# Sample attention of a hybrid decoder step: small matmuls moved into separate row and column tiles of the TensorE array

## The chip, the cores and the metric

The kernel is one program on one core of a Trainium2 chip. The metric is the device time in microseconds (us) of one execution; three runs of the kernel before gave 2195.8, 2200.24 and 2203.21, median 2200.24. Everything is computed in float32, in one launch.

## The reference, cut to what matters

The model is one inference step of a two-layer trunk: layer 0 with gated linear attention (GLA, four heads), layer 1 with sliding-window attention; in both a memory cross attention (four heads of 64) stands beside it, and SwiGLU feed-forward networks before and after. It runs on 512 prompt tokens and on 32 sample tokens (8 sequences of 4 new tokens, each sequence with its own past state or cache). The change is about three pieces of the work on the sample tokens:

```
# GLA, sample: per sequence b and head h, states S (96 x 192)
S = exp(g_t)[..., None] * S + k_t[..., :, None] * v_t[..., None, :]
o_t = einsum('bhk,bhkv->bhv', q_t, S)
# memory attention: keys and values of 256 memory tokens per sequence
s = einsum('blhd,bmhd->bhlm', q, mk) * 64 ** -0.5
o = einsum('bhlm,bmhd->blhd', softmax(s), mv)
```

The kernel computes the GLA recurrence of the four new tokens in closed form: output = (score matrix of the new tokens) times v, plus (decayed q) times the old state; new state = decay times old state plus (decayed k) transposed times v.

## The kernel before, in words

Activations stand transposed: features on the 128 partitions, tokens in the columns. Half 0 holds 256 prompt tokens and the 32 sample tokens (288 columns), half 1 the other 256. Dense products run on TensorE (PE) as three fp32r matmuls per block (`dense`, L356, and `product`, L342). The matmuls of the attention are float32 and each is two instructions on PE, so "x16" of such a line in the trace is eight matmuls.

Around the change the work of layer 0 is as follows. `in_a` projects half 0 to q, k, v and r; the v blocks are turned from features to tokens by transposes on PE (L805, 128 columns each; the sample block has 32 tokens). Then `weave` runs `attend_a` of half 0 (`attn_a` for GLA with `mem_prompt` and `mem_sample` for the memory heads) against a filler of dense work of half 1: the end of its first feed-forward, then its RMSNorm (`enter`: sums on PE at L400, `rstd`, a broadcast on PE at L412, the scaled and split inputs at L434, L298 and L299), then its own `in_a`. The filler's dense matmuls are what PE does while the attention waits, except between the last feed-forward product and the first projection, where the RMSNorm stands between them.

`attn_a` first makes the scores of the four heads (`gla_scores`; the decayed keys are turned at L929), then calls `gla_out` per head. There the prompt chunks come first (L953 to L966), then, for half 0, the sample part of that head, all of it on the 32 sample tokens:

- L976: eight masked copies of the keys (32 x 96 each, one per sequence), L980: eight masked copies of q (96 x 32).
- L983: one matmul scores x v, L990: eight matmuls masked q x old state, all into rows 0 to 31 of one PSUM bank (the stationary operand is 96 rows by 32 columns, 192 columns are streamed). The states are loaded for a pair of heads at the even head (L987), into eight buffers of the pool `ld`.
- L998: eight matmuls masked keys x v (32 rows by 96 columns, 192 streamed), L999: the new state on VectorE (DVE), and at the odd head its store (L1002).

`mem_sample` runs once per layer (l = 0 and 1). After the softmax, L715 masks the transposed probabilities of all four heads for one sequence, and L718 multiplies them (128 x 128) with the value block of all four heads (256 columns), 16 matmuls in all; of the 128 x 256 result only the four 32 x 64 diagonal blocks are kept (L724).

The order of the instructions on each engine is set when the kernel is built, by a scheduler that simulates the engines' times and takes priorities (`high_priority`); so an edit in one place moves instructions of other lines as well. On the chip each engine goes through its list in order and waits on semaphores.

Of the kernel before, what the change touches and what calls it, by code (L numbers as in the profile page):

```python
# [15 lines left out]
ALU = mybir.AluOpType  # L16
# [3 lines left out]
P = 128  # L20
# [36 lines left out]
def constants():  # L57
# [25 lines left out]
    bmt = (tok[:, None] // LS == np.arange(NB)[None]).astype(np.float32)  # L83
# [149 lines left out]
class Build:  # L233
# [126 lines left out]
    def copy(self, out, ps, scale=1.0):  # L360
        with self.tc.high_priority(offset=self.AHEAD):
            self.nc.scalar.activation(out, ps, AF.Copy, scale=scale)
        return out

# [311 lines left out]
    def mem_sample(self, l, mq, mo):  # L676
# [34 lines left out]
        for b in range(NB):  # L711
# [11 lines left out]
        for h in range(4):  # L723
            nc.scalar.activation(o[NS * h:NS * h + NS], po[NS * h:NS * h + NS, 64 * h:64 * h + 64], AF.Copy)  # L724
# [26 lines left out]
    def blocks(self, h):  # L751
        return ((0, P, 0), (P, P, 1)) + (((2 * P, NS, 2),) if h == 0 else ())

    def in_a(self, h, xs, s):
# [42 lines left out]
        for hp in range(2):  # L797
# [4 lines left out]
            for a, m, c in self.blocks(h):  # L802
                pv = self.bd() if h else self.bt()
                for j in range(3):
                    nc.tensor.transpose(pv[:m, j * P:(j + 1) * P], vf[j][:, a:a + m], self.ident)  # L805
                t = self.v("vtok")
                nc.scalar.activation(t[:m].rearrange("p a b -> p (a b)"), pv[:m, :2 * GV], AF.Copy)
# [13 lines left out]
    def attn_a(self, h, s):  # L821
# [7 lines left out]
        for i in range(GH):  # L829
            yield from self.gla_out(h, i, s, ss)  # L830
        s.tmp.close()
# [20 lines left out]
    def gla_scores(self, h, i, s):  # L852
# [75 lines left out]
        for a, n, c in self.blocks(h):  # L928
            nc.tensor.transpose(pk[:n, c * GK:(c + 1) * GK], kd[:, a:a + n], self.ident[:GK, :GK])  # L929
        nc.scalar.activation(kt[:, :2].rearrange("p a b -> p (a b)"), pk[:, :2 * GK], AF.Copy)  # L930
        if h == 0:
            nc.scalar.activation(kt[:NS, 2], pk[:NS, 2 * GK:3 * GK], AF.Copy)
# [4 lines left out]
    def gla_out(self, h, i, s, ss):  # L937
# [7 lines left out]
        def finish(po, n, c):  # L945
            nc.scalar.activation(o[c][:n], po, AF.Copy)
            junk = s.tmp.u(GV)
            nc.scalar.activation(junk[:n], po, AF.Square, accum_out=ss[:n, 4 * c + i:4 * c + i + 1])

        for c in range(2):  # L950
# [5 lines left out]
            finish(po[:, :GV], P, c)  # L956
# [11 lines left out]
        if h == 1:  # L968
            nc.sync.dma_start(d["o_gp"][i], self.state[i])
            self.drop(self.state[i], at, qe, kt)  # L970
            return

        kb, kbs = [], [self.u(shape=(2, GK), rows=NS) for _ in range(NB // 2)]
        for g in range(0, NB, 2):
            t = kbs[g // 2]
            nc.vector.tensor_tensor(out=t, in0=kt[:NS, 2].unsqueeze(1).to_broadcast([NS, 2, GK]),  # L976
                                    in1=self.bmt[:, g:g + 2].unsqueeze(2).to_broadcast([NS, 2, GK]), op=ALU.mult)
            kb += [t[:, 0], t[:, 1]]
        qb = self.u(shape=(NB, NS), rows=GK)
        nc.vector.tensor_tensor(out=qb, in0=self.bm[:GK], in1=qe[:, SC].unsqueeze(1).to_broadcast([GK, NB, NS]),  # L980
                                op=ALU.mult)
        po = self.bt()
        nc.tensor.matmul(po[:NS, :GV], ats, v[2][:NS], start=True, stop=False)  # L983
        for j in range(NB):
            if i % 2 == 0:
                st = self.ld("st", [P, 2, GV])[:GK]
                nc.sync.dma_start(st, d["state"][j, i // 2].rearrange("p (a v) -> p a v", a=2))  # L987
                self.st[j] = st
            st = self.st[j][:, i % 2, :]
            nc.tensor.matmul(po[:NS, :GV], qb[:, j, :], st, start=False, stop=j == NB - 1)  # L990
        finish(po[:NS, :GV], NS, 2)
        yield
        for j in range(0, NB, 2):
            pn = self.bt()
# [477 lines left out]
```

## Time and profile before

| | us |
|---|---|
| median of the three runs | 2200.24 |
| the profiled execution, its own time | 2195.54 |
| its span, first to last instruction | 2193.8 |
| PE busy in the span (share) | 2127.1 (97%) |
| DVE busy (share) | 1544.0 (70%) |
| ScalarE (ACT) busy (share) | 1067.2 (49%) |
| mean granted clock of TensorE | 0.981 of full speed |

The two sample attentions lie at 416 to 700 us (layer 0, half 0, woven with dense work of half 1) and at 1580 to 1720 us (layer 1). A PE instruction counts as busy from its start to the modelled end of its result, so consecutive ones overlap, and "busy" says that PE had something in flight, not that its array was full.

### The profile page before, as it was taken

Reading aid. Unit: us, or ns where it says so; the run is one execution under the profiler, and the core shown is the slowest. Engines: PE = TensorE matmul, PEld = TensorE weight load, DVE = VectorE, ACT = ScalarE, POOL = GpSimd, SP = SyncE. Lnnn points to the kernel's source line nnn. Section 1 sums busy time; section 2 is a strip of 40 time slices with the busy share of each in tenths; the row PEclk is TensorE's granted clock in tenths of the full one; section 3 lists DMA queues with packets and bytes.
Section 4 is the critical chain, followed back from the end, with each engine's and each line's share of the span. In section 5 each row is a group of like instructions: output and inputs, shape, how many; then the busy total and the mean of one; then the engine's idle time right before and its main releaser. Section 6 shows DMA issues by size and latency. Waiting matters only on the chain.

```text
span 2193.8 us, 40498 instructions
## 1 busy us (share of the span) xinstructions
PE 2127.1 (97%) x16166; PEld 2035.5 (93%) x16166; DVE 1544.0 (70%) x3246; ACT 1067.2 (49%) x2101; POOL 36.3 (2%) x69
## 2 busy tenths in 40 slices
PE   7999999999999998999999999999999999999998
PEld 6999999998789988999999999999987889999998
DVE  7886665587467868858577776665776876966755
ACT  5554444654446555525355554444443445544434
POOL 5000000000000000000000000000000000000000
PEclk9999999999899999999999999999999999999999
DMA  7533253434344432333354533243443333232344
GB/s 231 159 100 116 70 170 116 138 128 140 107 139 155 138 108 95 109 95 95 119 160 151 179 100 107 78 144 121 145 130 113 122 117 116 96 114 80 106 138 135
DMA packets 90398, 273.00 MB, mean 124 GB/s; under 512 B 11312, under 2 KB 25152, under 8 KB 90176
## 3 DMA queue, kind: packets, MB, share of 16 engines
q1 hardware_dynamic: 89632, 269.87, 39.1%
q8 instruction: 127, 2.08, 0.4%
q14 instruction: 63, 0.52, 0.1%
q10 hardware_dynamic: 576, 0.52, 0.1%
HBM read 264.04 MB, written 7.70 MB: 124 GB/s over the span
## 4 chain that ended last, share of the span: by engine, by line
PE 83%; DVE 8%; DMA 4%; issue 2%; ACT 1%; SPq 0%; DVEq 0%; ACTq 0%
PE bank L356 54%; PE bank L342 18%; PE bank L878 1%; PE bank L1103 1%; DMA u19r<-gu_ffn 1%; DMA u20r<-gu_ffn 1%; DMA u21r<-gu_ffn 1%; DMA u18r<-gu_ffn 1%; PE bank L645 1%; PE bank L998 1%; PE bank L990 1%; PE bank L1117 1%; PE bank L1116 1%; DVE u L299 1%; PE bank L666 1%
## 5 line engine op out<-in xcount | busy, mean ns | idle before, releaser
L298 ACT ACTIVATE u<-u 128x272 fp32r<-128x272 f32 (+3 forms) x328 | 133.3, 421 | 121.7 <-DVE u L533 47.6
L299 DVE TENSOR_TENSOR u<-u,u 128x272 fp32r<-128x272 f32 (+3 forms) x328 | 137.3, 429 | 8.2 <-ACT u L298 7.1
L541 DVE SCALAR_TENSOR_TENSOR x<-bank,x 128x16 f32<-128x16 f32 (+2 forms) x192 | 59.6, 342 | 115.4 <-PE bank L356 114.6
L356 PE MATMUL bank<-u,d0h 128*128 128x272 f32 (+2 forms) x352 | 71.6, 290 | 0.0
L356 PE MATMUL bank<-u,d1h 128*128 128x272 f32 (+2 forms) x352 | 70.8, 288 | 0.0
L356 PE MATMUL bank<-u,d2h 128*128 128x272 f32 (+2 forms) x352 | 68.4, 289 | 0.4 <-DVE x L741 0.4
L356 PE MATMUL bank<-u,d3h 128*128 128x272 f32 (+2 forms) x352 | 68.3, 290 | 0.0
L356 PE MATMUL bank<-u,d4h 128*128 128x272 f32 (+2 forms) x352 | 67.3, 288 | 0.0
L356 PE MATMUL bank<-u,d5h 128*128 128x272 f32 (+2 forms) x352 | 67.1, 288 | 0.0
L356 PE MATMUL bank<-u,d7h 128*128 128x272 f32 (+2 forms) x352 | 67.0, 288 | 0.0
L356 PE MATMUL bank<-u,d6h 128*128 128x272 f32 (+2 forms) x352 | 66.8, 288 | 0.0
L530 ACT ACTIVATE u<-u 128x272 f32<-128x272 f32 x56 | 24.1, 430 | 71.4 <-DVE u L529 71.4
L356 PEld LDWEIGHTS bank<-u,d0h 128*128 128x128 f32 x352 | 56.3, 188 | 0.2
L356 PEld LDWEIGHTS bank<-u,d1h 128*128 128x128 f32 x352 | 56.2, 188 | 0.0
L356 PEld LDWEIGHTS bank<-u,d2h 128*128 128x128 f32 x352 | 55.4, 188 | 0.7 <-issue 0.5
L356 PEld LDWEIGHTS bank<-u,d3h 128*128 128x128 f32 x352 | 55.5, 188 | 0.3 <-DVE x L576 0.3
L356 PEld LDWEIGHTS bank<-u,d4h 128*128 128x128 f32 x352 | 55.3, 188 | 0.4 <-issue 0.3
L356 PEld LDWEIGHTS bank<-u,d5h 128*128 128x128 f32 x352 | 55.1, 188 | 0.2
L356 PEld LDWEIGHTS bank<-u,d7h 128*128 128x128 f32 x352 | 55.1, 188 | 0.1
L356 PEld LDWEIGHTS bank<-u,d6h 128*128 128x128 f32 x352 | 55.2, 188 | 0.0
L356 PE MATMUL bank<-u,d1l 128*128 128x272 f32 (+2 forms) x176 | 50.8, 289 | 0.0
L356 PE MATMUL bank<-u,d4l 128*128 128x272 f32 (+2 forms) x176 | 50.7, 288 | 0.0
(1179 smaller groups left out, 7792.1 us busy)
## 6 DMA issues: line engine op xcount, KB each, us to landing
g0r<-gu_ffn SPq DMA_DIRECT2D x8, 512.0 KB, 3.3
u0r<-gu_ffn SPq DMA_DIRECT2D x8, 512.0 KB, 3.4
g1r<-gu_ffn SPq DMA_DIRECT2D x8, 512.0 KB, 3.5
u1r<-gu_ffn SPq DMA_DIRECT2D x8, 512.0 KB, 3.9
g2r<-gu_ffn SPq DMA_DIRECT2D x8, 512.0 KB, 3.4
u2r<-gu_ffn SPq DMA_DIRECT2D x8, 512.0 KB, 3.3
g3r<-gu_ffn SPq DMA_DIRECT2D x8, 512.0 KB, 3.4
u3r<-gu_ffn SPq DMA_DIRECT2D x8, 512.0 KB, 3.4
```

Source lines behind the costliest of these rows:

```text
L298: nc.scalar.activation(h, src, AF.Copy)
L299: nc.vector.tensor_tensor(out=l, in0=src, in1=h.bitcast(F32), op=ALU.subtract)
L342: self.nc.tensor.matmul(ps, a[:, k, :], x, start=start and k == 0 and j == 0, stop=k == len(xs) - 1 and j == 2, skip_group_check=True)
L356: self.nc.tensor.matmul(ps, w[:, k, :], x, start=i == 0 and j == 0, stop=i == kc - 1 and j == 2)
L530: nc.scalar.activation(c2, c2, AF.Silu)
L541: nc.vector.scalar_tensor_tensor(out=x, in0=p, scalar=0.5, in1=x, op0=ALU.mult, op1=ALU.add)
L645: nc.tensor.matmul(ps[:, b, :], mq[b][rows, tok], kt[b][rows], start=True, stop=True)
L666: nc.tensor.matmul(po[rows, (h // 2) * P:][:, :P], v[mt][:, 64 * h:64 * h + 64], pt[h][:, mt, :], start=mt == 0, stop=mt == 1)
L878: nc.tensor.matmul(pv[:, c * half:(c + 1) * half], lhs[:, c * P:(c + 1) * P], second(rhs[:, c * P:(c + 1) * P]), start=True, stop=True)
L990: nc.tensor.matmul(po[:NS, :GV], qb[:, j, :], st, start=False, stop=j == NB - 1)
L998: nc.tensor.matmul(pv[:, e], kb[j + e], v[2][:NS], start=True, stop=True)
L1103: nc.tensor.matmul(dst, self.vt[n - i][:, 64 * kv:64 * kv + 64], t.rearrange("p g t -> p (g t)"), start=i == 0, stop=i == last)
```

## The change

The matmuls of the three pieces are cut or regrouped so that neighbours in the instruction list use different row or column tiles of the array. `side_by_side` keeps the scheduler from reordering the TensorE instructions inside it among themselves.

- Memory heads: the 16 matmuls 128 x 128 by 256 columns per layer become 64 of 128 x 32 by 64 columns; four of them (one per head) write rows 0, 32, 64 and 96 of the same bank. The four copies of L724 become one.
- GLA, sample part: it leaves `gla_out` and becomes `gla_sample`, called once for two heads, after both heads' prompt parts. The q x state matmuls of the two heads alternate between column tiles (output rows 0 to 31 and 32 to 63). The masked keys now stand on all 128 partitions (the 32 tokens repeated four times), one mask per two groups of sequences, and the keys x v matmuls alternate between two row tiles and two PSUM banks. The second moment is taken from the copied output instead of PSUM.
- For this, the 32-token blocks of v and of the keys must stand four times on the partitions: `turn` replaces one transpose of such a block by four matmuls with the identity, into output rows 0, 32, 64 and 96.

```diff
+    def side_by_side(self):
+        return self.tc.manual_schedule(engines={self.nc.tensor.engine})
...
             for mt in range(2):
-                nc.tensor.matmul(po[:, :MT], pt[:, 4 * mt:4 * mt + 4].rearrange("p a t -> p (a t)"), vc[:, mt, :],
-                                 start=b == 0 and mt == 0, stop=b == NB - 1 and mt == 1)
+                with self.side_by_side():
+                    for h in range(4):
+                        nc.tensor.matmul(po[NS * h:NS * h + NS, :64], pt[:, 4 * mt + h, :], vc[:, mt, 64 * h:64 * h + 64],
+                                         start=b == 0 and mt == 0, stop=b == NB - 1 and mt == 1)
...
-        for h in range(4):
-            nc.scalar.activation(o[NS * h:NS * h + NS], po[NS * h:NS * h + NS, 64 * h:64 * h + 64], AF.Copy)
+        nc.scalar.activation(o, po[:, :64], AF.Copy)
...
+    def turn(self, out, t, ident):
+        m = t.shape[1]
+        if m == P:
+            self.nc.tensor.transpose(out, t, ident)
+        else:
+            with self.side_by_side():
+                for a in range(0, P, m):
+                    self.nc.tensor.matmul(out[a:a + m], t, ident, start=True, stop=True)
...
-                    nc.tensor.transpose(pv[:m, j * P:(j + 1) * P], vf[j][:, a:a + m], self.ident)
+                    self.turn(pv[:, j * P:(j + 1) * P], vf[j][:, a:a + m], self.ident)
...
             yield from self.gla_out(h, i, s, ss)
+            if h == 0 and i % 2:
+                yield from self.gla_sample(i // 2, s, ss)
...
+    def gla_sample(self, hp, s, ss):
+        nc, d = self.nc, self.d
+        v, o = s.v[2, hp], s.o[2, hp]
+        st, kb, qb = [], [], []
+        for j in range(NB):
+            t = self.ld("st", [P, 2, GV])[:GK]
+            nc.sync.dma_start(t, d["state"][j, hp].rearrange("p (a v) -> p a v", a=2))
+            st.append(t)
+        heads = s.heads[2 * hp:2 * hp + 2]
+        for at, ats, qe, kt, eb_last in heads:
+            kb.append(self.u(shape=(2, GK)))
+            nc.vector.tensor_tensor(out=kb[-1], in0=kt[:, 2].unsqueeze(1).to_broadcast([P, 2, GK]),
+                                    in1=self.bmt.unsqueeze(2).to_broadcast([P, 2, GK]), op=ALU.mult)
+            qb.append(self.u(shape=(NB, NS), rows=GK))
+            nc.vector.tensor_tensor(out=qb[-1], in0=self.bm[:GK], in1=qe[:, SC].unsqueeze(1).to_broadcast([GK, NB, NS]),
+                                    op=ALU.mult)
         po = self.bt()
+        out = [po[NS * e:NS * e + NS, :GV] for e in range(2)]
+        for e in range(2):
+            nc.tensor.matmul(out[e], heads[e][1], v[:NS, e], start=True, stop=False)
+        with self.side_by_side():
+            for j in range(NB):
+                for e in range(2):
+                    nc.tensor.matmul(out[e], qb[e][:, j, :], st[j][:, e, :], start=False, stop=j == NB - 1)
...
+        for jj in range(2):
+            for r0 in (0, 2):
+                js = [r0 + r + 4 * jj for r in range(2)]
+                pn = [self.bt()[:GK, :2 * GV].rearrange("p (a v) -> p a v", a=2) for _ in js]
+                with self.side_by_side():
+                    for e in range(2):
+                        for r in (1, 0):
+                            rows = slice(NS * (r0 + r), NS * (r0 + r) + NS)
+                            nc.tensor.matmul(pn[r][:, e], kb[e][rows, jj], v[rows, e], start=True, stop=True)
+                for j, p in zip(js, pn):
+                    for e in range(2):
+                        nc.vector.scalar_tensor_tensor(out=st[j][:, e], in0=st[j][:, e], scalar=heads[e][4][:, 2 + j:3 + j],
+                                                       in1=p[:, e], op0=ALU.mult, op1=ALU.add)
+                    nc.sync.dma_start(d["o_gs"][j, hp].rearrange("p (a v) -> p a v", a=2), st[j])
```

In the changed file L724 is the memory heads' matmul, L767 the four-fold turn, L1003, L1007 and L1021 are the scores x v, q x state and keys x v matmuls, L1024 the new state, and L404, L416, L438 and L719 stand for L400, L412, L434 and L715.

On PE, at the RMSNorm of half 1 in layer 0, the list before is this (L400 sums, L953 a prompt part, L412 the broadcast):

```order
L400 MATMUL bank_68<-ones,u_6235 128x1
L998 MATMUL bank_72<-vtok,u_6394 96x192
L998 MATMUL bank_71<-vtok,u_6393 96x192
L990 MATMUL bank_70<-st,u_6624 32x192 x8
L953 MATMUL bank_72<-vtok,u_5450 128x192
L998 MATMUL bank_71<-vtok,u_6396 96x192
L412 MATMUL bank_69<-u_6296,ones 128x128 x2
```

The same place in the changed list, between the last sum and the broadcast:

```order
L404 MATMUL bank_68<-ones,u_6286 128x1
L1007 MATMUL bank_71<-st,u_6515 32x192
L1007 MATMUL bank_71<-st,u_6519 32x192
L1021 MATMUL bank_70<-vtok,u_6513 96x192
L1007 MATMUL bank_71<-st,u_6515 32x192
L1021 MATMUL bank_72<-vtok,u_6513 96x192
L1007 MATMUL bank_71<-st,u_6519 32x192
L1021 MATMUL bank_70<-vtok,u_6517 96x192
L1007 MATMUL bank_71<-st,u_6515 32x192
L1021 MATMUL bank_72<-vtok,u_6517 96x192
L1007 MATMUL bank_71<-st,u_6519 32x192
L416 MATMUL bank_69<-u_6352,ones 128x128 x2
```

Eight q x state matmuls of one head stood ahead of the broadcast; now the last six of a pair of heads do, and four of them alternate with four keys x v matmuls, each time with another tile shape.

On DVE, just after the diagonal for that broadcast is made, the list before begins the normalised inputs (L434) behind two state updates and goes on in turns:

```order
L410 TENSOR_SCALAR u_6296<-c_ident,r 128x128 x2
L999 SCALAR_TENSOR_TENSOR st<-st,ebl,bank_71 96x192
L999 SCALAR_TENSOR_TENSOR st<-st,ebl,bank_70 96x192
L434 SCALAR_TENSOR_TENSOR u_6303<-x_493,gains,u_6301 128x256
L434 SCALAR_TENSOR_TENSOR u_6309<-x_495,gains,u_6301 128x256
L963 SCALAR_TENSOR_TENSOR u_6581<-u_6573,ebl,bank_72 96x192
```

In the changed list the same inputs (there L438) come behind four state updates, the scaling of the memory softmax (L707, L708) and three masked copies of its transposed probabilities (L719):

```order
L414 TENSOR_SCALAR u_6352<-c_ident,r 128x128 x2
L707 RECIPROCAL ssm<-ssm 128x1
L1024 SCALAR_TENSOR_TENSOR st<-st,ebl,bank_70 96x192 x2
L708 TENSOR_SCALAR u_6735<-u_6735,ssm 128x256
L1024 SCALAR_TENSOR_TENSOR st<-st,ebl,bank_72 96x192 x2
L719 TENSOR_TENSOR u_6929<-bank_73,c_bm 128x256
L719 TENSOR_TENSOR u_6947<-bank_73,c_bm 128x256
L719 TENSOR_TENSOR u_7099<-bank_73,c_bm 128x256
L438 SCALAR_TENSOR_TENSOR u_6359<-x_493,gains,u_6357 128x256
L438 SCALAR_TENSOR_TENSOR u_6365<-x_495,gains,u_6357 128x256
L299 TENSOR_TENSOR u_6362<-u_6359,u_6361 128x256
```

So memory work that stood behind the first inputs now stands ahead of them.

## Rows read from the trace of the kernel before

**Rows 1.** The page's first part (busy time, share of the span, instructions) and its chain of waits: shares of the span by engine, then by line.

```profile
PE 2127.1 (97%) x16166; PEld 2035.5 (93%) x16166; DVE 1544.0 (70%) x3246; ACT 1067.2 (49%) x2101; POOL 36.3 (2%) x69
...
PE 83%; DVE 8%; DMA 4%; issue 2%; ACT 1%; SPq 0%; DVEq 0%; ACTq 0%
```

**Rows 2.** Busy time by stretch: from:to in us, length, then per engine the busy us and the instructions, then the granted clock, DMA share and GB/s.

```profile
500.00:542.00 42.00, 42.00 (x328) 38.09 (x327) 28.30 (x69) 18.98 (x45) 0.00 (x0) 1.00 0.41 126
542.00:592.00 50.00, 49.09 (x219) 32.20 (x218) 25.23 (x66) 19.53 (x57) 0.00 (x0) 0.83 0.41 127
592.00:640.00 48.00, 47.39 (x305) 38.51 (x304) 28.31 (x65) 26.95 (x59) 0.00 (x0) 0.96 0.38 116
...
1656.00:1678.00 22.00, 18.70 (x112) 14.07 (x109) 17.45 (x68) 9.33 (x32) 0.00 (x0) 1.00 0.35 111
```

**Rows 3.** The chain of work in order of time, layer 0: start us, us that the piece holds the chain, engine, tile, line, instructions.

```profile
546.32 5.26 PE bank L990 x16
...
552.52 0.88 PE bank L998 x2
553.40 1.15 PE bank L412 x4
...
566.45 0.86 PE bank L718 x4
...
570.33 0.44 PE bank L990 x2
...
582.88 4.93 DMA o_gs<-st
...
609.63 2.72 PE bank L990 x16
...
613.20 0.49 PE bank L998 x2
```

**Rows 4.** PE groups by line over the whole span: tiles, shape, count, busy us, mean ns of one, idle before.

```profile
L998 PE MATMUL bank<-vtok,u 32*96 32x192 f32 x64 | 19.1, 393 | 0.5 <-DVE st L999 0.5
L718 PE MATMUL bank<-mvc,u 128*128 128x256 f32 x64 | 17.1, 391 | 0.6 <-ACT u L298 0.6
L990 PE MATMUL bank<-st,u 96*32 96x192 f32 x64 | 15.0, 380 | 0.4 <-DMA st<-state 0.4
```

**Rows 5.** PE in order of time, from several windows: start us, us from the first start to the last end, engine, line, tiles, rows * columns of the stationary operand, moving operand, instructions.

```profile
423.64 0.49 PE L805 MATMUL bank<-c_ident,u 128*128 128x128 f32 x3
...
1606.82 1.05 PE L1169 MATMUL bank<-sck,u 64*128 64x128 f32 x8
...
1611.31 1.16 PE L1169 MATMUL bank<-sck,u 64*128 64x128 f32 x16
...
1635.56 1.10 PE L1214 MATMUL bank<-stc,scv 128*64 128x16 f32 x16
...
1657.04 1.08 PE L692 MATMUL bank<-mkc,u 128*64 128x256 f32 x8
...
1672.27 1.99 PE L718 MATMUL bank<-mvc,u 128*128 128x256 f32 x8
```

**Rows 6.** The instructions of single lines: count, duration in ns (least/median/most), first and last start, shape.

```profile
L692 PE MATMUL bank<-mkc,u x64: 379/380/687, 486.9 to 1659.2; 128*64 128x256 f32 x64
...
L1169 PE MATMUL bank<-sck,u x48: 271/272/373, 1600.6 to 1619.5; 64*128 64x128 f32 x32, 128*128 128x128 f32 x16
...
L1214 PE MATMUL bank<-stc,scv x32: 209/209/230, 1635.6 to 1638.4; 128*64 128x16 f32 x32
```

**Rows 7.** DVE and ACT in order of time around the broadcast of half 1's RMSNorm: start us, us, engine, line, operation, tiles, shape, count, idle before and what ended it.

```profile
547.88 0.48 DVE L410 TENSOR_SCALAR u<-c_ident,r 128x128 f32<-128x128 f32 x2
553.44 0.41 DVE L999 SCALAR_TENSOR_TENSOR st<-st,ebl,bank 96x192 f32<-96x192 f32 x1 [5.08 <-PE bank L998]
...
555.81 0.87 DVE L434 SCALAR_TENSOR_TENSOR u<-x,gains,u 128x256 f32<-128x256 f32 x2
...
570.38 0.42 DVE L299 TENSOR_TENSOR u<-u,u 128x256 fp32r<-128x256 f32 x1
...
554.59 0.38 ACT L417 ACTIVATE u<-bank 128x256 f32<-128x256 f32 x1 [1.39 <-PE bank L412]
```

**Rows 8.** Short stretches with the granted clock (columns as in rows 2).

```profile
542.00:544.00 2.00, 2.00 (x15) 1.23 (x13) 1.74 (x6) 1.95 (x4) 0.00 (x0) 1.00 0.78 264
...
546.00:548.00 2.00, 2.00 (x8) 1.03 (x7) 1.93 (x11) 0.00 (x0) 0.00 (x0) 0.50 0.75 262
...
560.00:562.00 2.00, 2.00 (x8) 1.93 (x8) 1.47 (x5) 0.72 (x4) 0.00 (x0) 0.50 0.31 83
...
1644.00:1648.00 4.00, 4.00 (x13) 2.62 (x14) 1.34 (x5) 0.79 (x4) 0.00 (x0) 0.50 0.00 0
```

**Rows 9.** DVE and ACT groups of the sample work (columns as in rows 4).

```profile
L976 DVE TENSOR_TENSOR u<-u,c_bmt 32x192 f32<-32x192 f32 x16 | 5.4, 340 | 2.8 <-PE bank L990 2.5 <-PE bank L356 0.2
L999 DVE SCALAR_TENSOR_TENSOR st<-st,ebl,bank 96x192 f32<-96x192 f32 x32 | 12.8, 405 | 21.3 <-PE bank L998 21.2
L715 DVE TENSOR_TENSOR u<-bank,c_bm 128x256 f32<-128x256 f32 x16 | 6.4, 418 | 6.6 <-PE bank L718 5.1 <-PE bank L707 1.4
...
L724 ACT ACTIVATE u<-bank 32x64 f32<-32x64 f32 x8 | 1.7, 215 | 3.9 <-issue 3.4 <-PE bank L718 0.4
...
L932 ACT ACTIVATE u<-bank 32x96 f32<-32x96 f32 x4 | 0.9, 224 | 0.0
```

More of the change, by code (lines that the diff above doesn't have):

```diff
@@ L928, in gla_scores @@
         for a, n, c in self.blocks(h):
[L929 to L932, printed above, removed]
+            self.turn(pk[:, c * GK:(c + 1) * GK], kd[:, a:a + n], self.ident[:GK, :GK])
+        nc.scalar.activation(kt[:, :c + 1].rearrange("p a b -> p (a b)"), pk[:, :(c + 1) * GK], AF.Copy)
         s.heads[i] = at, ats, qe, kt, eb_last
@@ L943, in gla_out @@
         o = [s.o[c, i // 2][:, i % 2, :] for _, _, c in self.blocks(h)]
[L945 to L948, printed above, removed]
         for c in range(2):
@@ L955, in gla_out @@
                 nc.tensor.matmul(po[:, :GV], qe[:, c * P:(c + 1) * P], state, start=False, stop=True)
-            finish(po[:, :GV], P, c)
+            nc.scalar.activation(o[c], po[:, :GV], AF.Copy)
+            nc.scalar.activation(s.tmp.u(GV), po[:, :GV], AF.Square, accum_out=ss[:, 4 * c + i:4 * c + i + 1])
             pn = self.bt()
@@ L970, in gla_out @@
             self.drop(self.state[i], at, qe, kt)
[L971 to L979, printed above, removed]
@@ L980, in gla_out @@
-        nc.vector.tensor_tensor(out=qb, in0=self.bm[:GK], in1=qe[:, SC].unsqueeze(1).to_broadcast([GK, NB, NS]),
-                                op=ALU.mult)
-        po = self.bt()
[L983 to L990, printed above, removed]
@@ L991, in gla_out @@
-        finish(po[:NS, :GV], NS, 2)
-        yield
-        for j in range(0, NB, 2):
-            pn = self.bt()
-            pv = pn[:GK, :2 * GV].rearrange("p (a v) -> p a v", a=2)
-            for e in range(2):
-                st = self.st[j + e][:, i % 2, :]
-                nc.tensor.matmul(pv[:, e], kb[j + e], v[2][:NS], start=True, stop=True)
-                nc.vector.scalar_tensor_tensor(out=st, in0=st, scalar=eb_last[:, 2 + j + e:3 + j + e],
-                                               in1=pv[:, e], op0=ALU.mult, op1=ALU.add)
-                if i % 2:
-                    nc.sync.dma_start(d["o_gs"][j + e, i // 2].rearrange("p (a v) -> p a v", a=2), self.st[j + e])
-            if j == NB - 2:
-                self.drop(at, qe, kt, qb, kbs)
-            yield
+    def gla_sample(self, hp, s, ss):
[14 more added lines that the diff above has]
+                                    op=ALU.mult)
+        po = self.bt()
+        out = [po[NS * e:NS * e + NS, :GV] for e in range(2)]
[6 more added lines that the diff above has]
+        for e in range(2):
+            at = 8 + 2 * hp + e
+            nc.scalar.activation(o[:NS, e], out[e], AF.Copy)
+            nc.scalar.activation(s.tmp.u(GV, rows=NS), o[:NS, e], AF.Square, accum_out=ss[:NS, at:at + 1])
+        yield
+        for jj in range(2):
[8 more added lines that the diff above has]
+                for j, p in zip(js, pn):
+                    for e in range(2):
+                        nc.vector.scalar_tensor_tensor(out=st[j][:, e], in0=st[j][:, e], scalar=heads[e][4][:, 2 + j:3 + j],
+                                                       in1=p[:, e], op0=ALU.mult, op1=ALU.add)
+                    nc.sync.dma_start(d["o_gs"][j, hp].rearrange("p (a v) -> p a v", a=2), st[j])
+                if js[-1] == NB - 1:
+                    self.drop([t for e in heads for t in (e[0], e[2], e[3])], kb, qb)
+                yield
@@ L1327, in run @@
         self.mr = None
-        self.vt, self.state, self.st = [None] * 5, [None] * GH, [None] * NB
+        self.vt, self.state = [None] * 5, [None] * GH
         self.x = [[], []]
```

4 lines of the change are left out of this document (2 added, 2 removed).

## The prediction

> **What bounds the kernel now.** I read the page's first part and its chain first, then stretches of the two sample attentions, then the chain inside them, then single lines. The first shows PE busy for 97% of the span and holding 83% of the chain that ended last, DVE 8%, DMA 4% [rows 1]. Since a busy PE may be half empty, the stretches matter more. Where the change lies in layer 0, PE is busy for 42.0 of 42, 49.1 of 50 and 47.4 of 48 us, DVE and ACT for about half [rows 2]. So PE's list sets the pace there, and a microsecond less in it should be nearly a microsecond less in the end. Layer 1 is looser: 18.7 of 22 us [rows 2].
>
> Inside, the chain walks over the sample matmuls themselves. Eight q x state matmuls hold it for 2.72 us in one place and for 5.26 us in another, and the broadcast L412 stands in the list behind the second of these [rows 3]. [...]
>
> **What is removed.** In the chain one matmul (two instructions) costs: L990 0.34 us in a row of eight (2.72 / 8), 0.44 alone; L998 0.49 alone, 0.88 at half clock; L718 0.43 (0.86 / 2) [rows 3]. L990: 2.72 + 5.26 + 2.72 + 8 alone x 0.44 = 14.2 us. L998: 32 matmuls, 6 of them at half clock, 26 x 0.48 + 6 x 0.88 = 17.8. L718: 32 x 0.44 = 14.1, half in each layer. L983: 4 x 0.44 = 1.8. Together 47.9 us. The busy times of the three larger groups are a little higher, 19.1, 17.1 and 15.0 us, since they count tails that lie beside the next matmul [rows 4].
>
> **What is added.** Does work in two tiles lie side by side here? Two pairs of rows say yes for two tiles. L718, on the whole array, gives eight instructions of 256 columns in 1.99 us. L692, same columns, alternating between two column tiles of 64, gives eight in 1.08 [rows 5]. Without the last one's own 0.38 us [rows 6], starts are 0.23 and 0.10 us apart. For row tiles, L1169 gives 8 instructions in 1.05 us when one tile is used and 16 in 1.16 when two alternate [rows 5]. The second tile is free in both.
>
> Four tiles are not shown, nor anything as short as 64 columns in them. Bounds, per instruction:
> - q x state (L1007): 32 matmuls, 16 pairs. A free second tile gives 16 x 0.34 = 5.4 us, none gives 32 x 0.38 = 12. The last six of the first pair of heads alternate with keys x v matmuls of another tile shape, so they go as if alone. I take 6.5.
> - keys x v (L1021): 32 in 8 groups of two pairs. A pair at the pace of one: 0.33 (192 columns at L1169's 0.111 us for 128, twice) to 0.41; a change of shape costs 0.10 (0.44 against 0.34 for L990). Bounds 5.4 and 32 x 0.49 = 15.7. I take 8 x (0.74 + 0.10) = 6.7.
> - scores x v (L1003): four as before, 1.8.
> - Memory heads (L724): 32 groups of four matmuls, 8 instructions each, 256 in all. If all four tiles are free, a group costs two instructions of 64 columns, 0.108 us (a quarter of L718's 0.43), so 3.5 in all. From above, the fastest steady rate of short instructions in this trace is L1214's (1.10 - 0.21) / 15 = 0.059 us [rows 5, 6]; at that 8 cost 0.47, 15.1 us in all. I take 0.25 per group, 8.0, between them and nearer the rows in which another tile was free.
> - Four-fold turns (L767): 10 groups of four, 8 instructions each, in place of one of 0.11 us ((0.49 - 0.27) / 2 for L805, with 0.27 as the tail of a 128-column instruction, L1169's) [rows 5, 6]. Net +0.1 to +0.8 each; I take +0.25, 2.5 us.
>
> [...]
>
> So PE has 6.5 + 6.7 + 1.8 + 8.0 + 2.5 = 25.5 us where it had 47.9, 22.4 less. With every lower bound the gain is 47.9 - 17.1 = 31, with every upper one 47.9 - 52.6 = -5.
>
> Beside PE: 16 masks L976 of 0.34 us become 4, 12 x 0.34 = 4.1 us less DVE; six copies of 0.215 and four of 0.224 fewer on ACT, 2.2 us less [rows 9]. Both lie beside PE and count nothing. The state loads of the second pair wait in SP's list for the first pair's stores as before; the one place where PE came late for that (a store of 4.93 us on the chain [rows 3]) falls away, because the second pair's matmuls now come after two heads of prompt work.
>
> **How much of it arrives.** Four places:
> - 416 to 542: one row of eight L990 (2.72), five L998 and an L983 leave (5.6 us together), turns enter (+2.5): 3.1 us gained.
> - 542 to 592: of the sample work here (two L983 0.9, L990 8.8, L998 9.3, L718 7.0, together 26) some 12 remain (scores x v 0.9, q x state 3.7, keys x v 3.4, memory 4.0), 14 less. But this is where half 1's RMSNorm has to finish before dense work returns. The diagonal L410 is done at 548.4, the broadcast runs at 553.4 and the first inputs come at 555.8 [rows 3, 7], so at most 5 us can be won ahead of the broadcast. After it the changed DVE list puts four state updates (0.41 each), a scaling and three masked copies (0.42 each) ahead of the first input, 3.2 us that stood behind it, and PE's memory matmuls wait for the same copies. I also expect half clock there again, since the stretch still has no dense work: 2 us more for what runs in it. Of 14 I count 10.
> - 592 to 640: L983 0.4, L990 2.7 and some 15 L998 (7.3) become 7.1: 3.4 gained.
> - Layer 1: 7.0 becomes 4.0; DVE and loads leave PE idle there, so 2 of the 3 count.
>
> Sum 18.5 us. The profiled execution's own time is 2195.54, span 2193.8 and 1.7 around it; 2195.5 - 18.5 = 2177. It lies 4.7 below the median of the runs shown, so I predict 2182 for a median.
>
> **Rivals.**
> - Four tiles go at the pace of the list, 0.059 us per instruction: the memory heads cost 15.1 (+7.1) and the turns 10 x 0.37 net more (+1.2, to 3.7). Gain 18.5 - 8.3, of which a part was behind waits anyway: 10 us, 2190. For: no steady rate above it in the trace. Against: neighbours in different tiles were free, so far as two go. [...]
> - The wait takes over at 542 to 592: the DVE list behind the broadcast (3.2 us moved ahead, and each group of keys x v needs two of three banks, which DVE gives back after 4 x 0.41 us) holds PE, and the 10 us become 2. Gain 10, also 2190. For: DVE's idle 5.08 us there ended by L998 [rows 7] show how tightly the two lists are coupled. Against: DVE is busy 25 of 50 us [rows 2].
> - Slower: the clock. Narrow matmuls alone were followed by 0.50 twice, at 546 and at 1644 [rows 8]. If the packed pieces keep it at half through 562 to 592 and through layer 1's memory heads, then some 25 us of dense and sample work at full speed take 50, +25 against -18: 2207. It decides from about 18 us of full-speed work at half. Against: with more narrow work in it, 542 to 592 still had a mean of 0.83 before [rows 2].
> - The tiles do nothing: each matmul at its own pace, upper bounds, +5, less the 5 us of half clock that the row of eight L990 cost: 2200. L692 and L1169 speak against it.
>
> **Chances.** Forecast with its own range (gain 12 to 26, 2174 to 2188) 0.52; list pace 0.21; wait 0.12; slower 0.06; nothing 0.04; a gain over 26 us 0.05. The range for 8 in 10 takes the forecast, both cases near 2190 and some of the rest: 2168 to 2197. About 0.3%, 6.6 us, is what a measurement of this kernel can tell, so faster means under 2193.6. Faster: 0.52 + 0.05 + two thirds of 0.33 = 0.79, of which I give 0.02 up for a median that reads high: 0.77. Within 0.3%: the other third and most of "nothing", 0.16. Slower 0.07.
>
> **What would show it.** Right: groups of L724 under 0.3 us; sixteen L1007 matmuls in a row near 2.9 us; the broadcast L416 less than 9 us after the first sums; 542 to 592 shortened by about 10 us; PE still busy above 95%. Wrong: L724 at 0.45 us or more per group (list pace); PE idle behind DVE L719 or L1024 (wait); a granted clock of 0.5 over more than the 20 us of before (clock). The forecast falls if the time before half 1's first projection does not shrink although the sample matmuls do.

## The result, and the profile after

The kernel after takes 2189.65 us (median of five runs, 2185.2 to 2190.97), the kernel before 2200.24 (five runs on the same chip): ratio 0.9947, 95% interval 0.9927 to 0.9967. A second comparison on one chip gave 2190.35 against 2198.95, 0.9953 (0.9935 to 0.9970). So the gain is 10 to 12 us by the ratios (9 to 11 by the medians) where 18 were forecast. The direction held, and so did the whole range, 2168 to 2197; the narrower range of the forecast itself, 2174 to 2188, was missed by 1.7 us. The profiled execution of after took 2186.22 us, its span is 2184.4.

Line numbers moved: the sums of the RMSNorm are now L404, its broadcast L416, the masks of the memory heads L719.

The page's first part and the chain by engine, of after (before: [rows 1]):

```profile
PE 2112.6 (97%) x16428; PEld 2030.0 (93%) x16428; DVE 1538.9 (70%) x3234; ACT 1066.5 (49%) x2091; POOL 35.7 (2%) x69
...
PE 89%; DVE 6%; ACT 2%; DMA 2%; issue 1%; SPq 0%; DVEq 0%; ACTq 0%
```

PE still holds most of the chain (89%), and its busy time fell by 14.5 us.

The stretches of layer 0, of after, with the columns of [rows 2]:

```profile
500.00:542.00 42.00, 41.39 (x347) 39.14 (x346) 29.08 (x71) 20.86 (x47) 0.00 (x0) 1.00 0.50 149
542.00:592.00 50.00, 48.49 (x426) 37.33 (x427) 30.17 (x79) 31.80 (x86) 0.00 (x0) 0.86 0.43 133
592.00:640.00 48.00, 47.09 (x361) 43.31 (x361) 29.72 (x58) 23.43 (x40) 0.00 (x0) 1.00 0.51 161
```

Against [rows 2], twice as many PE instructions go through in 542 to 592 (x426 for x219). That is not only the finer cut: dense matmuls (L356) among them are 141 for 72. And the third stretch runs at 1.00 instead of 0.96.

The chain of waits in order of time, of after, layer 0 (start us, us, engine, tile, line, instructions; answers to [rows 3]):

```profile
543.04 1.75 PE bank L1007 x20
544.79 0.76 PE bank L404 x6
...
546.49 0.44 PE bank L1007 x2
...
547.87 0.50 PE bank L1021 x2
548.37 0.78 PE bank L1007 x2
...
550.81 1.15 PE bank L416 x4
...
558.08 3.59 DMA mvc<-mv
...
562.45 3.14 PE bank L356 x14
...
566.63 0.82 PE bank L1021 x8
567.46 0.45 PE bank L724 x18
...
584.75 2.72 PE bank L1007 x32
```

Sixteen q x state matmuls (x32) now take the 2.72 us that eight took in [rows 3]: the second column tile is free. Four keys x v matmuls take 0.82. Eighteen of the short memory instructions take 0.45, 0.025 us each, far below the 0.059 that was the fastest steady rate in the trace of before. Where q x state and keys x v alternate one by one, one of q x state costs 0.44 at full clock, as alone before [rows 3], and 0.78 at half: nothing is saved there, where its neighbour has another tile shape. In a row in one tile one took 0.34 [rows 3], and in the long row in two 2.72 / 16 = 0.17. What takes the difference isn't shown.

The granted clock in that stretch, of after (columns as in [rows 8]):

```profile
540.00:548.00 8.00, 7.38 (x56) 4.45 (x55) 4.03 (x14) 5.55 (x11) 0.00 (x0) 1.00 0.40 134
548.00:558.00 10.00, 10.00 (x82) 6.99 (x82) 7.28 (x22) 3.36 (x11) 0.00 (x0) 0.51 0.35 98
562.00:566.00 4.00, 4.00 (x35) 3.83 (x28) 2.21 (x7) 0.05 (x1) 0.00 (x0) 0.59 0.69 205
```

Half clock (a granted clock of 0.50) comes again after the narrow matmuls, but for about 14 us, where before had it from 546 to 562 [rows 8] and once more near 594 (0.96 over 592 to 640, [rows 2]).

Where the time went is seen best from the dense matmuls, which are the same in all kernels. The table gives, for the dense matmuls that start near a time of the first profile of before, how much later (+) or earlier (-) they start in another profile, in us. (Median over the matmuls that start in the 25 us from that time on; "before 2", "after 2" and "after 3" are profiles of the unchanged kernels taken again; the other columns are experiments below.)

```
near us   before 2  after  after 2  after 3   e1    e2     e3     e4
  400       1.3      0.0    -0.5      0.1    1.6   -1.0   -0.6    0.5
  475       1.3      2.8     2.2      2.9    1.6    1.8    2.1    3.3
  550       1.4     -5.4    -5.7     -5.3    2.2   -3.1   -6.0    7.4
  600       4.7    -17.9   -16.8    -17.6   -0.7  -14.5  -18.5   -0.7
  650       4.7    -19.8   -18.7    -19.4   -1.8  -18.2  -20.4   -7.9
 1150       3.5    -17.2   -17.1    -14.0   -3.5  -17.4  -16.7   -6.5
 1250       8.2    -14.0   -15.3    -10.6    1.1  -15.7  -11.8   -3.4
 1600       5.8    -14.3   -15.8    -10.6    0.7  -14.9  -11.6   -3.4
 1700       8.4    -11.3   -10.6     -9.3    4.8   -9.4   -3.2    1.0
 2175       7.0    -10.2   -10.4     -9.6    5.3  -10.0   -3.9    2.2
```

Layer 0 alone wins 19 to 20 us by 650. Then some is given back: 3 to 9 us by 1600, and 1 to 5 more at layer 1's attention (1600 to 1700). What gives it back was the open question.

### The profile page after: what moved, and what is told of

It is laid out like the page before. It is cut to its first block, busy times and chain, and to the rows that moved or that the text cites. A ratio compares the mean times of both kernels' runs of the same rounds, so it can differ in the third digit from the quotient of the medians.

```text
span 2184.4 us, 41000 instructions
## 1 busy us (share of the span) xinstructions
PE 2112.6 (97%) x16428; PEld 2030.0 (93%) x16428; DVE 1538.9 (70%) x3234; ACT 1066.5 (49%) x2091; POOL 35.7 (2%) x69
## 4 chain that ended last, share of the span: by engine, by line
PE 89%; DVE 6%; ACT 2%; DMA 2%; issue 1%; SPq 0%; DVEq 0%; ACTq 0%
PE bank L356 54%; PE bank L342 25%; PE bank L1126 1%; PE bank L895 1%; PE bank L649 1%; PE bank L1140 1%; PE bank L1139 1%; PE bank L670 1%; DVE u L299 0%; PE bank L416 0%; PE bank L404 0%; PE bank L696 0%; DMA mvc<-mv 0%; PE bank L1007 0%; PE bank L1161 0%
## 5 line engine op out<-in xcount | busy, mean ns | idle before, releaser
L298 ACT ACTIVATE u<-u 128x272 fp32r<-128x272 f32 (+2 forms) x328 | 133.2, 421 | 122.6 <-DVE u L537 50.8
L299 DVE TENSOR_TENSOR u<-u,u 128x272 fp32r<-128x272 f32 (+2 forms) x328 | 137.2, 428 | 3.7 <-ACT u L298 2.2
L356 PE MATMUL bank<-u,d0h 128*128 128x272 f32 (+2 forms) x352 | 71.0, 289 | 0.0
L356 PE MATMUL bank<-u,d1h 128*128 128x272 f32 (+2 forms) x352 | 70.7, 288 | 0.0
L356 PE MATMUL bank<-u,d2h 128*128 128x272 f32 (+2 forms) x352 | 68.0, 289 | 0.4 <-DVE x L746 0.4
L356 PE MATMUL bank<-u,d3h 128*128 128x272 f32 (+2 forms) x352 | 67.8, 289 | 0.0
L356 PE MATMUL bank<-u,d5h 128*128 128x272 f32 (+2 forms) x352 | 67.8, 289 | 0.0
L356 PE MATMUL bank<-u,d4h 128*128 128x272 f32 (+2 forms) x352 | 67.5, 289 | 0.0
L356 PE MATMUL bank<-u,d6h 128*128 128x272 f32 (+2 forms) x352 | 67.4, 288 | 0.0
L356 PE MATMUL bank<-u,d7h 128*128 128x272 f32 (+2 forms) x352 | 67.1, 288 | 0.0
L356 PEld LDWEIGHTS bank<-u,d0h 128*128 128x128 f32 x352 | 56.2, 188 | 0.1
L356 PEld LDWEIGHTS bank<-u,d1h 128*128 128x128 f32 x352 | 56.1, 188 | 0.0
L356 PEld LDWEIGHTS bank<-u,d2h 128*128 128x128 f32 x352 | 55.2, 188 | 0.6 <-issue 0.5
L356 PEld LDWEIGHTS bank<-u,d3h 128*128 128x128 f32 x352 | 55.4, 188 | 0.3 <-DVE x L580 0.3
L356 PEld LDWEIGHTS bank<-u,d5h 128*128 128x128 f32 x352 | 55.3, 188 | 0.2
L356 PEld LDWEIGHTS bank<-u,d4h 128*128 128x128 f32 x352 | 55.2, 188 | 0.2
L356 PEld LDWEIGHTS bank<-u,d6h 128*128 128x128 f32 x352 | 55.3, 188 | 0.0
L356 PEld LDWEIGHTS bank<-u,d7h 128*128 128x128 f32 x352 | 55.1, 188 | 0.1
L356 PE MATMUL bank<-u,d7l 128*128 128x272 f32 (+2 forms) x176 | 50.9, 289 | 0.0
L356 PE MATMUL bank<-u,d1l 128*128 128x272 f32 (+2 forms) x176 | 50.8, 289 | 0.0
```

The lines of the kernel that those rows point to most:

```text
L298: nc.scalar.activation(h, src, AF.Copy)
L299: nc.vector.tensor_tensor(out=l, in0=src, in1=h.bitcast(F32), op=ALU.subtract)
L356: self.nc.tensor.matmul(ps, w[:, k, :], x, start=i == 0 and j == 0, stop=i == kc - 1 and j == 2)
```

## The experiments

Theory 1 at the start: the tiles are nearly free, but in layer 1 the shorter memory matmuls only uncover DVE's list and the loads. This is what stands there in after, the chain in order of time:

```profile
1650.49 1.41 PE bank L724 x48
1651.92 4.37 DMA mvc<-mv
...
1660.09 0.85 PE bank L416 x4
...
1663.15 0.96 PE bank L356 x5
```

After the first 24 memory matmuls the chain passes to the loads of the values, and the first dense matmul comes only when all of them are done. The broadcast L416 stands behind seven of their eight groups here; in the list before, L412 stood behind four. The rivals: the memory heads win as forecast and something else loses; or the granted clock differs from execution to execution (theory 2).

**e1, e2, e3: which part of the change gives what.** e1 is before with the memory heads alone cut into four tiles (its edit is the part on `mem_sample` in the diff ahead of the prediction). e2 is after with the memory heads as before, e3 has them as before in layer 1 only:

```diff
             for mt in range(2):
-                with self.side_by_side():
-                    for h in range(4):
-                        nc.tensor.matmul(po[NS * h:NS * h + NS, :64], pt[:, 4 * mt + h, :], vc[:, mt, 64 * h:64 * h + 64],
+                nc.tensor.matmul(po[:, :MT], pt[:, 4 * mt:4 * mt + 4].rearrange("p a t -> p (a t)"), vc[:, mt, :],
```

> The kernel before with only the memory heads cut into four column tiles, both layers; GLA's sample part and the turns as before. Theory 1 (the four tiles are nearly free, but in layer 1 the shorter matmuls only uncover the value loads and DVE's list, and give 3.5 us back there): layer 0 wins 2 to 4 us, layer 1 loses 3 to 4, in all 2197 to 2202. Rival (the memory heads win in both layers, and the shortfall comes from order elsewhere): 2192 to 2195.

> The kernel after with the memory heads of both layers as before (16 matmuls of 256 columns per layer); GLA's sample part and the turns as after. Theory 1: it keeps most of layer 0's gain and doesn't give back the 3.5 us of layer 1, so 2185 to 2190, level with the kernel after or a little faster. Rival (the memory heads carry a share of the gain as forecast, 4 us in layer 0 and 2 in layer 1): 2194 to 2197.

> The kernel after, with layer 1's memory heads alone as before; layer 0's stay in four tiles. Theory 1: the dense work behind layer 1's memory heads comes 3 to 5 us earlier than in the kernel after, 2184 to 2187. Rival (what is lost at 1640 to 1670 us isn't due to the cut matmuls, but to a shift that the rest of the program would show as well): 2189 to 2191.

Measured, each against before on the same chip (2199.77): e1 2201.19, ratio 0.9998 (0.9983 to 1.0013); e2 2188.57, 0.9944 (0.9924 to 0.9964); e3 2188.43, 0.9945 (0.9923 to 0.9966). So the GLA part carries the whole gain, 12.3 us by e2's ratio (8 to 17), and the memory heads give 0.4 us (3.7 faster to 2.9 slower). e1 and e2 came as theory 1 expected. e3 did not: it is no faster than after, and its dense matmuls lose 8.4 us at layer 1 (-11.6 to -3.2 in the table) although its memory matmuls there are those of before; e2 loses 5.5. After itself loses 3.0, 5.2 and 1.3. So theory 1 falls: what is lost in layer 1 is lost without the cut matmuls as well.

**e4: do the neighbours make the gain?** The same pieces in an order in which neighbours share a tile:

```diff
-            for j in range(NB):
-                for e in range(2):
+            for e in range(2):
+                for j in range(NB):
                     nc.tensor.matmul(out[e], qb[e][:, j, :], st[j][:, e, :], start=False, stop=j == NB - 1)
...
-                    for e in range(2):
-                        for r in (1, 0):
+                    for r in (1, 0):
+                        for e in range(2):
...
-            for mt in range(2):
-                with self.side_by_side():
-                    for h in range(4):
+            with self.side_by_side():
+                for h in range(4):
+                    for mt in range(2):
```

> The kernel after with the same pieces in another order, so that neighbours share a tile: all eight q x state matmuls of one head, then of the other; keys x v with both heads of one row tile in a row; the memory heads' two value blocks of one head in a row. Theory (what was won is the second and fourth tile side by side): q x state 32 x 0.17 = 5 us longer, keys x v 32 x 0.15 = 5 us, memory heads 64 x 0.05 to 0.1 = 3 to 6 us, in all 2198 to 2206. Rival (fewer streamed columns, fewer masks and the grouping of two heads make the gain, not the neighbours): 2188 to 2192.

Measured 2201.61 us, 1.0002 (0.9988 to 1.0017): the whole gain is gone, and the time lies in the theory's range. PE in order of time, of e4 (start us, us from the first start to the last end, engine, line, tiles, rows * columns of the stationary operand, moving operand, instructions, idle before):

```profile
579.98 1.81 PE L1007 MATMUL bank<-st,u 96*32 96x192 f32 x10
...
584.45 2.46 PE L1007 MATMUL bank<-st,u 96*32 96x192 f32 x14
...
589.99 0.90 PE L1021 MATMUL bank<-vtok,u 32*96 32x192 f32 x8
...
1664.93 1.27 PE L724 MATMUL bank<-mvc,u 128*32 128x64 f32 x48 [0.56 <-ACT u L298]
...
1671.81 0.45 PE L724 MATMUL bank<-mvc,u 128*32 128x64 f32 x16
```

and of after, the same view:

```profile
566.56 0.89 PE L1021 MATMUL bank<-vtok,u 32*96 32x192 f32 x8
...
584.68 2.79 PE L1007 MATMUL bank<-st,u 96*32 96x192 f32 x32
...
1650.49 1.36 PE L724 MATMUL bank<-mvc,u 128*32 128x64 f32 x48 [0.56 <-issue]
...
1660.87 0.45 PE L724 MATMUL bank<-mvc,u 128*32 128x64 f32 x16
```

Fourteen instructions of q x state take 2.46 us where 32 took 2.79 with a neighbour in the other tile, both at full clock (no L1007 of e4 lasts over 0.35 us; those of after at half clock last up to 0.53). Counted on PE from each instruction's start to the next one's, L1007 takes 11.3 us in layer 0 (7.4 in after); 3.9 us are what the neighbours are worth there. The other two pieces are another matter. A group of four keys x v matmuls takes 0.90 us in e4 and 0.89 in after. Of the memory heads the two rows of 48 can't be compared, since that of after ran at half clock for the most part:

```profile
1650.50:1651.90 1.40, 1.36 (x48) 1.10 (x48) 1.40 (x6) 0.25 (x2) 0.00 (x0) 0.58 0.00 0
```

The rows of sixteen, at full clock, take 0.45 us in both (in after those at half clock take 0.66). So for these two a tile repeated once costs nothing that shows, and the expected 5 and 3 to 6 us were wrong; that the time came as the theory had it is luck.

What else e4 loses, it loses in layer 0 too: 11 to 12 us by 650 in the table (-7.9 against -18.7 to -19.8). By the same count L1021 takes 10.7 us (9.4) and L724 7.6 (5.2) there, with waits. The scheduler had moved other lines as well. This is the chain of e4 behind the broadcast, in order of time:

```profile
555.38 1.29 DVE st L1024 x4
...
557.00 0.79 DVE u L438 x2
...
566.03 0.65 DVE st L1024 x2
...
567.79 0.65 PE bank L724 x10
...
569.95 1.37 PE bank L356 x5
```

From 555 to 567.7 the chain is on DVE, where the normalised inputs (L438) stand between state updates and masks, and 542 to 592 has a mean clock of 0.83; in after 14 dense instructions in a row hold the chain from 562.45. So e4 shows 3.9 us for the neighbours in q x state. How much of the rest is due to the order of the pieces, and how much to the other lines that moved with it, it doesn't show.

**e5, e6: the unchanged kernels, profiled again.**

> The kernel before, unchanged, profiled a second time. All four kernels so far, also those with layer 1's memory heads as before, lost 3 to 9 us against the profile of before at 1640 to 1660 us, with 24 to 32 us at half clock there against its 10. Theory 2 (the stretch at half clock behind layer 1's narrow matmuls differs from execution to execution, and the profile of before had a short one): more than 18 us at half clock there now, and the dense work behind it 3 to 8 us later than in the first profile, in all 2198 to 2207. Theory 1's remainder (the changed kernels lose it themselves): the same 10 us, 2195 to 2197.

> The kernel after, unchanged, profiled a second time. Theory 2: the stretches at half clock lie in the same places (layer 0's sample part, layer 1's, one or two at 1160 to 1230 us) but not of the same length, and the time moves with them by 2 to 5 us; the shift against before up to 650 us stays 18 to 20. Rival: the same lengths within 1 us.

The second profile of before took 2202.88 us, 7.3 more than the first. The table shows where: 3.4 us near 600, 4.7 between 1150 and 1250, 2.6 in layer 1, and 1.2 to 2.4 us the other way in between. In 1160 to 1240 almost nothing but dense work is on PE. Its rows, columns as in [rows 2]; first profile of before, with layer 1 below:

```profile
1160.00:1240.00 80.00, 76.13 (x588) 74.85 (x588) 65.30 (x141) 45.83 (x83) 0.00 (x0) 1.00 0.52 163
1620.00:1665.00 45.00, 42.57 (x293) 32.45 (x293) 28.17 (x107) 15.27 (x58) 0.73 (x3) 0.89 0.37 118
```

second profile of before:

```profile
1160.00:1240.00 80.00, 76.12 (x556) 74.84 (x555) 59.78 (x128) 41.85 (x74) 0.00 (x0) 0.94 0.51 162
1620.00:1665.00 45.00, 45.00 (x305) 35.42 (x303) 27.84 (x98) 15.41 (x54) 0.73 (x3) 0.81 0.38 120
```

first profile of after:

```profile
1160.00:1240.00 80.00, 76.00 (x555) 74.71 (x554) 62.35 (x135) 44.29 (x83) 0.00 (x0) 0.96 0.49 151
1620.00:1665.00 45.00, 38.88 (x337) 26.40 (x337) 23.35 (x94) 13.17 (x54) 0.00 (x0) 0.73 0.35 107
```

and e2, whose PE list in this attention is that of before but for a few instructions moved by one to six places:

```profile
1620.00:1665.00 45.00, 42.82 (x216) 28.48 (x215) 23.09 (x91) 11.19 (x42) 0.00 (x0) 0.70 0.34 106
```

PE was busy for 76.1 of the 80 us in both profiles of before and did 588 instructions in the one, 556 in the other. If the clock is either 1.00 or 0.50, as in the short stretches of [rows 8], a mean of 0.94 stands for an estimated 80 x 2 x 0.06 = 9.6 us at half. In layer 1, (1 - clock) x 2 x 45 gives 10, 17, 24 and 27 us at half clock for these four. So theory 2 holds in this: the stretches at half clock differ between executions of one kernel, and the first profile of before, on which the forecast stands, had few. Between 1150 and 1250 they account, by the estimate that follows, for all that is lost. If half of the time at half clock is lost (eight q x state matmuls took 2.72 us at full and 5.26 at half clock, [rows 3]), the loss is an estimated (1 - clock) x 80 us: 4.8 us for the second profile of before (4.7 in the table) and 3.2 for the first of after (3.2). Theory 2 came short in size: 17 us and 2.6 us later where over 18 and 3 to 8 were expected. And after's second profile differs from its first in the clock (0.70 in layer 1, 0.98 in 1160 to 1240) but only by 0.2 us in time, where 2 to 5 had been expected.

**e7, e8: dense work among the narrow matmuls.** e7 weaves five more units of half 1's work into layer 1's attention, e8 does that and four in layer 0; the numbers are the third of each tuple (units held back):

```diff
-    FILL = ((6, 1, 7, 2, 6), (7, 2, 5, 0, 9))
+    FILL = ((6, 1, 7, 2, 6), (7, 2, 0, 0, 9))   # e7
+    FILL = ((6, 1, 3, 2, 6), (7, 2, 0, 0, 9))   # e8
```

> The kernel after, but in layer 1 five more units of half 1's work are woven into the attention of half 0, so that half 1's RMSNorm stands before the memory heads' masks in DVE's list and its projection's dense matmuls stand among the memory heads' matmuls. Theory 1 and 2 alike (narrow matmuls in a row bring half clock, and PE waits for the value loads there): idle time of PE at 1648 to 1660 gone, half clock there under 10 us, 4 to 8 us faster than after, 2182 to 2186. Rival (PE is busy for 97% anyway and the order within it makes no difference): 2188 to 2192.

> As the one before, and in layer 0 four more units of half 1's work in the attention of half 0, so that the broadcast stands ahead of the q x state matmuls and dense matmuls between the keys x v ones. If half clock is what holds back layer 0: its 14 us at half clock fall under 7, 3 to 5 us faster than with layer 1 alone, 2178 to 2183. If not: the same as with layer 1 alone within 2 us.

e7 missed both of its ranges: 2193.91 us, 0.9964 (0.9949 to 0.9978). e8, 2195.73, 0.9989 (0.9970 to 1.0007), missed the hoped-for one and is level with e7 within 2 us, as its second one said. The interval of e8 lies above that of after; that of e7 overlaps it. In layer 0 the half clock did go: e8's 542 to 592 ran at 1.00 with 478 instructions, and its dense matmuls near 600 are 25.6 us early, 8 more than in after. But at 1150, where its dense matmuls come in the others' order again, it is 17.6 us early and after 17.2, so nothing of the 8 is left. And e7, 20.6 us early near 1650, is 2.2 us late near 1700 and 3.8 early at the end, where after is 10.2 early. What PE waited for: e7, 1655 to 1740 us (engine, line, waited for: us in total, times, longest):

```profile
PE bank L416 <- DVE u L414: 3.3, 1, 3.3
```

e8, 600 to 700 us:

```profile
PE bank L356 <- DVE u L830: 4.3, 1, 4.3
PE bank L763 <- ACT u L362: 2.1, 2, 1.2
```

So the dense work that was pulled forward is missing where it stood: behind e8's attention PE waits for the normalised heads (L830; 1.1 us in after), in e7 for the next RMSNorm, and e7's 1720 to 1740 then ran at 0.68:

```profile
1720.00:1740.00 20.00, 18.94 (x91) 15.57 (x92) 14.70 (x55) 9.01 (x32) 0.00 (x0) 0.68 0.00 0
```

**e9 to e12: how far to go in layer 0.** After itself, and after with the third number of layer 0's tuple at 6, 5 and 4 instead of 7 (one, two and three units more in the attention):

```diff
-    FILL = ((6, 1, 7, 2, 6), (7, 2, 5, 0, 9))
+    FILL = ((6, 1, 6, 2, 6), (7, 2, 5, 0, 9))   # e10; e11: 5, e12: 4
```

> The kernel after, unchanged, timed beside the three kernels below on one chip: 2187 to 2191. Its profile is a third one; theory 2: 650 us is reached 18 to 21 us earlier than in the first profile of before, and the stretches at half clock at 1160 to 1240 and 1620 to 1665 have other lengths than in the first two.

> The kernel after, with one more unit of half 1's work woven into layer 0's attention (the broadcast then stands between the first q x state matmuls, and dense matmuls between all groups of keys x v). If half clock in layer 0 costs time (theory 2): less than 7 us at half clock at 540 to 600 against 14, 2 to 4 us faster than after. Rival (the dense work woven in earlier is missing where the attention ends, as in the kernel with four units): 0 to 3 us slower than after.

> As the one before with two units. Theory 2: less than 5 us at half clock at 540 to 600, 2 to 5 us faster than after. Rival: PE waits over 3 us for the normalised heads before the output projection, level with after or slower.

> As the one before with three units. Theory 2: no half clock at 540 to 600, 2 to 5 us faster than after. Rival: the loss at 640 to 700 that four units showed (10 us) begins here, 2190 to 2196.

Measured against before (2198.95): e9 2190.35, 0.9953 (0.9935 to 0.9970); e10 2190.02, 0.9956 (0.9942 to 0.9971); e11 2185.46, 0.9934 (0.9911 to 0.9957); e12 2188.30, 0.9943 (0.9921 to 0.9965). The stretches 540 to 570 and 650 to 700 of e10:

```profile
540.00:570.00 30.00, 25.39 (x281) 19.43 (x283) 18.98 (x54) 14.40 (x41) 0.00 (x0) 1.00 0.46 144
...
650.00:700.00 50.00, 45.91 (x344) 45.23 (x343) 38.96 (x99) 29.05 (x57) 1.33 (x6) 0.90 0.47 151
```

e9 came as expected in time and at 650 us (19.4 earlier); its clock was that of after's first profile in 1160 to 1240 (0.96) and higher in 1620 to 1665 (0.77). The half clock of layer 0 is gone in e10 with a single unit, as expected, but it comes back at 650 to 700 (0.90, after had 0.97), where PE is busy for less of the time (45.9 us, after 46.8), and the total is that of after, so the 2 to 4 us didn't come. e11 and e12 came in their time, 4.9 and 2.1 us faster than after. But e12 had some 14 us at half clock (0.93 in 542 to 592 and again in 592 to 640), where none was expected, so its time doesn't speak for theory 2. e11 has the lowest median of all kernels here; its interval and that of after overlap, so it isn't shown to beat after. It is 0.7% faster than before.

## Why the prediction was right, and where it wasn't

- **PE's list sets the pace in layer 0**: right. 16.5 us were forecast for the three places of layer 0 together (3.1, 10 and 3.4), and the dense matmuls near 650 are 18.7 to 19.8 us earlier than in the first profile of before. The split among the three was not as forecast: 1.6 us by 525 for 3.1, 16.3 from there to 600 for 10 (-1.6 to -17.9), 1.9 from there to 650 for 3.4. That the sum came near is in part luck.
- **The price of the pieces**: nearly right in sum. From start to next start over 416 to 700 us, in the trace of after: L1007 7.4 us (6.5 forecast), L1021 9.4 (6.7), L724 5.2 with its waits (4.0), L1003 0.9 (1.8), the turns 3.5 in place of 0.5, so 3.0 more (2.5). That is 25.9 for 21.5. L1021 is the one that was sized too low: its first four matmuls stand alone between those of L1007, and some ran at half clock (up to 631 ns for a median of 321). By the same count the removed lines had 14.2, 17.8, 7.1 and 1.8, so 15.0 us less work on PE. That 19 arrived I put down, as an estimate, to the shorter half clock: 14 us after for some 20 before ([rows 8] and the 0.96 of [rows 2]), half of the difference, of which a part is in the 15.0 already.
- **The signs named**: L724 in groups of eight at 0.2 us (0.45 / 18 x 8), under 0.3; sixteen L1007 in 2.72, near 2.9; the broadcast 5.3 us after the sums (545.55 to 550.81), under 9; 542 to 592 shortened by 16 us, over the 10; PE busy for 97%. All came as written for the forecast or better.
- **The failing step** is "Layer 1: 7.0 becomes 4.0; ... so 2 of the 3 count". With their share of layer 0 the memory heads were 2 + 3 x 10 / 14 = 4.1 of the 18.5 us; e1 measured 0.4 (3.7 faster to 2.9 slower). In the table e1 does win 3.4 us in layer 0 (1.6 to -1.8) but loses 4.1 in layer 1 (0.7 to 4.8), and after loses 1 to 5 there instead of winning 2. The GLA part, 14.4 in the sum, measured 12.3 in e2 (8 to 17) and is within its interval.
- **A second one** is unspoken: the sum takes the rest of the program as equal in both kernels. The table contradicts it: between 650 and 1600 three profiles of after give back 5.5, 2.9 and 8.8 us and the second profile of before 1.1; e5 shows that a stretch of dense work differs by 4.7 us between two executions of one kernel. That the sum carries the 4.7 us between before's profile and its median over was nearly right: two profiles of after lie 3.4 and 3.5 us below the medians beside them.
- **Rivals.** The pace of the list (2190) has the measured time by chance: its mechanism falls with 0.025 us per instruction, and in the trace of after four short instructions at 567.4 us start only 7, 7 and 6 ns apart. The wait (also 2190) put its loss at 542 to 592, which won more than forecast. "The tiles do nothing" falls with the 2.72 us for sixteen q x state matmuls, where eight took as long. "Slower: the clock" failed in layer 0, where half clock got shorter (14 us for some 20). In layer 1 it was longer than in both profiles of before (20 us or more against 10 and 17), but after lost only 1 to 5 us there, and the rival's 25 didn't come.
- **Open**: why the changed kernels give back 3 to 9 us between 650 and 1600 and before's second profile only 1. Between 1150 and 1250 it is the clock, by the estimate made with e5: 0.96, 0.98 and 0.96 in 1160 to 1240 give 3.2, 1.6 and 3.2 us for the three profiles of after, and the table has 3.2, 1.8 and 3.4. What they lose before 1150 (2.6, 1.6 and 5.4 us) isn't explained. In layer 1 the profiles of after and of e1 to e4 had some 21 us or more at half clock, e2's too, whose list is nearly that of before; two profiles of before are too few to tell whether it, too, has them mostly. This wasn't tried further.

## What to carry to other kernels

A row of matmuls of few columns cost half here when neighbours in the list used different tiles of one shape: sixteen of q x state took the 2.72 us of eight. Alternating one by one between two tile shapes gave it away again (0.44 us each). Two in a row in one tile cost nothing that showed (in e4 0.90 us for after's 0.89 in keys x v, 0.45 for 0.45 in the memory heads). An experiment that changes the order of a few instructions can move the whole list, as e4 did, so see what else moved before its time is called the price of the order. Where a stretch without dense work ended in half clock, weaving dense work into it brought the clock back in two experiments (542 to 592 at 1.00 in e8, 540 to 570 at 1.00 in e10; 0.86 and 0.77 in after), not in a third (0.93 over 542 to 592 in e12). But the dense work was then missing at the next pause (4.3 us of waiting in e8), so watch the end of the stretch as well. And before a forecast is built on one profile, look at a second one of the same kernel: here they differ by 7.3 us, two thirds of the gain.

## What was unexpected of the hardware

The granted clock after a short pause of PE wasn't the same in two executions of one kernel (1.00 and 0.50). In 1160 to 1240 both profiles of before have the same two pauses, of 1.1 us (from 1179.7 and from 1183.2 us) and of 2.8 us some 45 us later, with dense work on either side. Around the first pause, first profile:

```profile
1180.00:1184.00 4.00, 3.21 (x23) 2.85 (x24) 1.81 (x5) 3.00 (x7) 0.00 (x0) 1.00 0.76 237
1184.00:1188.00 4.00, 4.00 (x33) 4.00 (x32) 1.78 (x5) 2.14 (x2) 0.00 (x0) 1.00 0.11 41
```

second profile:

```profile
1182.00:1186.00 4.00, 2.89 (x21) 2.24 (x19) 2.19 (x5) 2.78 (x6) 0.00 (x0) 0.95 0.54 158
1186.00:1192.00 6.00, 6.00 (x26) 6.00 (x27) 1.30 (x7) 0.98 (x2) 0.00 (x0) 0.50 0.26 90
```

In the first PE goes on at 1.00 with 33 matmuls in 4 us, in the second at 0.50 with 26 in 6 us, which cost 3.1 us by the table's finer steps (from 3.5 to 6.6 us late). The second pause goes the same way: no half clock in the first profile (1.00 over all of 1160 to 1240), and 1.6 us more lost in the second. The runs show the two outcomes; what decides between them they don't show.
